# Three weight sums per Strassen step instead of four: the first made by an adding transfer in the raw slot, the last two in one operation; four raw slots and a ring of 2 KB cells

## The chip, the cores and the metric

The kernel runs on one core of a Trainium2 chip. Its time is in microseconds (us) of the device, from the first to the last instruction and what lies around them, as the median of several runs. Three runs of the kernel before gave 2356.12 to 2356.76 us, median 2356.58. One more execution was taken by the profiler, and all tables come from it. The engines have short names: PE multiplies matrices, DVE works on vectors, ACT evaluates functions and also copies, POOL and SP here mostly issue transfers (DMAs).

## What is computed

One decoder block over 256 tokens of width 4096, all in float32. Nearly all of its work is four kinds of matrix product with weights that are read once:

```python
h = rmsnorm(x, norm_w)
proj = h @ w_in                       # 4096 x 20480
u_p, z_p, u_c, b_c, c_c, z_c, g_logit = split(proj)
y_pool = causal_multiscale_pool(u_p, pool_w, pool_scale) * silu(z_p)
y_conv = causal_gated_shortconv(u_c, b_c, c_c, conv_w, conv_b) * silu(z_c)
br = [y_pool @ w_branch[0], y_conv @ w_branch[1]]      # each 2048 x 4096
gates = sigmoid(g_logit + gate_b)
x = x + (gates[0] * br[0] + gates[1] * br[1]) @ w_out  # 4096 x 4096
return rmsnorm(x, final_norm_w)
```

## The kernel before

**Numbers in two parts.** PE multiplies numbers of type fp32r, which have fewer bits than float32. Each operand is therefore split into a high part (rounded to fp32r) and a low part (what rounding took away), and each product is made of three: high by high, high by low, low by high.

**Units and steps.** The output is made in units of 256 tokens by 1024 columns: conv branch (cz, cb, cu, cc), pool branch (pz, pu), eight gate units (g), eight branch units (b), four output units (o0 to o3). A unit sums over 16 steps (a branch unit over 8). One step is one block of weights, 128 partitions by 2048 float32, 1 MB: a 2 by 2 block matrix of quarters with 512 columns each, numbered 0 to 3 along the partition's row.

A step is plain (P) or Strassen (S). P takes 8 block products of 3 matmuls, 24 in all. S takes 7, so 21, but on the weight side it needs sums of quarters, which must be formed and split into parts as well. On the side of x the sums Q3, Q5, Q6, Q7 are kept in SBUF (`sums_s`, L767). A text for each unit sets the kinds: the middle gate units follow `TEN = "PSPSSPSSPSSPSSPS"` (L42), ten S steps to six P. The whole program has 222 S steps.

**Banks.** Products with quarters 0 and 1 and the last sum go to the banks called sums, the others to four banks called shared. At a unit's end ACT copies the shared banks to the tile J (`copy_corners`, L410), DVE forms three sums there (`corner_sums`, L415: two of 128x512 and one of 128x1024), and these are added to the unit's result E or Y (`combine`, L425). For units marked late that addition is done by two DMAs of POOL, `gather` (L84): a gather reads a source and adds it to what stands at its destination.

**Preparing a step.** SP loads the block into one of `NRAW = 3` raw slots (`issue_load`, L976). `first` (L256) has ACT write the high parts into cells of the ring (`highs`, L231): four for P, quarters 0 to 2 for S. `rest` (L277) has DVE write the low parts (`lows`, L235). For S, `added` (L293) forms four sums on DVE in the tile sums, which the profile calls parts, and `split` (L301) writes their high and low parts. The ring has 15 cells; each holds a high and a low part of 512 columns, 4 KB per partition. Cells are given out in a circle and released after the last matmul that reads them.

**What sets the order.** The whole program is written out in one fixed order: every helper pins its instruction behind the one before it on its engine. `multiply` (L1021) emits a group of three matmuls; after each group `after_group` copies what is finished, lets `tick` (L1014) take a small piece of other work, and calls `pump` (L988). The pump emits the preparation of later steps, up to `AHEAD = 4` steps ahead, as long as the ring has room; it emits the load of block n as soon as block n-3 has been prepared, and on SP that load then waits until DVE is through with the slot. POOL has no computing to speak of: it issues stores, reloads and gathers, in program order.

In the profile the DVE helpers are all L61, ACT's activations L58, SP's loads L76, POOL's plain DMAs L82 and gathers L85, and the matmuls L1026.

Of the kernel before, what the change touches and what calls it, by code (L numbers as in the profile page):

```python
# [9 lines left out]
F32 = mybir.dt.float32  # L10
# [16 lines left out]
CELLS = 15  # L27
NRAW = 3
# [22 lines left out]
def hybrid_block(ctx: ExitStack, tc: tile.TileContext, x, xc, prm, rows_in, w_in, pool_w, w_branch, w_out, out):  # L51
# [49 lines left out]
    ring = blocks("ring", [P, CELLS, 2, NH], F32R)  # L101
    E = blocks("E", [P, 2, NU])
    sa = blocks("sa", [P, 8, P])
# [126 lines left out]

    def highs(cells, src):  # L231
# [7 lines left out]
    def high(cell, a=0, b=NH):  # L239
        return ring[:, cell, 0, a:b]  # L240

    def low(cell, a=0, b=NH):
        return ring[:, cell, 1, a:b]
# [4 lines left out]
    class Step:  # L248
# [7 lines left out]
        def first(self):  # L256
# [3 lines left out]
            def rounded(cells):  # L260
                self.q = self.raw.rearrange("p (i c) -> p i c", i=4)
                self.cells = cells
                if self in steps[:2]:
                    for i in range(4):
                        if self is steps[0] and i == 0:
                            copy(ring[:, cells[0], 0], self.q[:, 0])
                        else:
                            highs(cells[i:i + 1], self.q[:, i:i + 1])
                elif self.halved:
                    for i in (0, 2):  # L270
                        highs(cells[i:i + 2], self.q[:, i:i + 2])
                else:
                    highs(cells, self.q[:, 0:len(cells)])

            return [(3 if self.kind == "S" else 4, None, rounded)]

        def rest(self):  # L277
            if self.kind == "P":
                def rests(_):
                    if self in steps[:2]:  # L280
                        for i in range(4):
                            if self is steps[0] and i % 2 == 0:
                                x_low(0, 1 - i // 2)
                            lows(self.cells[i:i + 1], self.q[:, i:i + 1])
                    elif self.halved:
                        for i in (0, 2):
                            lows(self.cells[i:i + 2], self.q[:, i:i + 2])
                    else:
                        lows(self.cells, self.q)

                return [(None, None, rests)] + self.mid
            if self.kind == "S":
                def added(_):  # L293
                    q = self.q
                    add(sums[:, 0:2], q[:, 3:4].to_broadcast([P, 2, NH]), q[:, 1:3])
                    lows(self.cells[2:3], q[:, 2:3])
                    add(sums[:, 2], sums[:, 0], q[:, 2])
                    lows(self.cells[0:2], q[:, 0:2])
                    add(sums[:, 3], sums[:, 2], q[:, 0])

                def split(cells):  # L301
                    self.sum_cells = cells
                    highs(cells[0:2], sums[:, 0:2])
                    for i in (2, 3):
                        highs(cells[i:i + 1], sums[:, i:i + 1])
                    lows(cells[0:2], sums[:, 0:2])
                    lows(cells[2:4], sums[:, 2:4])

                return [(None, None, added)] + self.mid + [(4, None, split)]
            if self.kind == "B":  # L310
                def parts(cells):
                    self.cells = cells
                    highs(cells, quarters(E))
                    lows(cells, quarters(E))

                return [(4, lambda: self.unit.flags.get("base"), parts)]

            def pooled(cells):
                self.pool_cells = cells
                q = quarters(E)[:, 2 * self.g:2 * self.g + 2]  # L320
                highs(cells, q)
                lows(cells, q)

            return [(None, None, lambda _: lows(self.cells, self.q)),
                    (2, lambda: self.unit.flags.get(f"pooled{self.g}"), pooled)]

        def groups(self):
            gs = []
            if self is steps[0]:
                for k in (1, 0):  # L330
                    for n in (1, 0):
                        cell = self.cells[2 * (1 - k) + 1 - n]
                        h, l = high(cell), low(cell)
# [4 lines left out]
                        gs[-1][2] = [cell]  # L338
            elif self.kind == "P":
                for k in (1, 0):  # L340
                    for n in reversed(self.halves):
                        cell = self.cells[2 * (1 - k) + 1 - n]
                        for t in self.toks:
                            ah, al = self.op.standing(k, t)
                            gs.append([("E", t, n), [(ah, high(cell)), (ah, low(cell)), (al, high(cell))], ()])
                        if self.final:
                            gs[-1][2] = [cell]
            else:
                d, w = self.cells, self.sum_cells
                prods = {"M1": (A11, d[2], ("F", 0, 0)),  # L350
                         "N3": (Q3, d[1], ("E", 0, 0)),
                         "M2": (A12, d[0], ("E", 0, 1)),
                         "N5": (Q5, w[1], ("F", 0, 1)),
                         "N7": (Q7, w[0], ("F", 1, 0)),
                         "N6": (Q6, w[2], ("F", 1, 1)),
                         "N4": (A22, w[3], ("E", 1, 1))}
                order = ("M2", "N3", "N4", "M1", "N7", "N5", "N6") if self.closing else (
                    "M2", "N3", "M1", "N7", "N5", "N6", "N4")
                for nm in order:
                    o, cell, bank = prods[nm]  # L360
                    ah, al = self.op.entry(o)
                    mm = [(ah, high(cell)), (ah, low(cell)), (al, high(cell))]
                    gs.append([bank, mm, [cell]])
# [280 lines left out]
    def band_sums(st):  # L644
        c = st.band
        for b in range(8):
            g = b // 4
            o = shared(b // 2)[:, (b % 2) * T:(b % 2 + 1) * T]
            c0, c1 = st.cells[g], st.cells[2 + g]
            ab = (b % 4) * P, (b % 4 + 1) * P  # L650
            bands, edge = band_pool["bands"], band_pool["edge"]
            pin(nc.tensor.matmul(o, high(c0, *ab), bands[:, g], start=True, stop=False))  # L652
            pin(nc.tensor.matmul(o, low(c0, *ab), bands[:, g], start=False, stop=False))  # L653
# [593 lines left out]
```

## Time and profile before

| | busy us | share of the span | instructions |
|---|---|---|---|
| PE | 2340.7 | 99% | 10424 |
| DVE | 2217.8 | 94% | 2454 |
| ACT | 1542.9 | 66% | 1841 |
| POOL | 139.0 | 6% | 195 |
| span of the profiled execution | 2354.7 | | 28337 |
| median of three runs | 2356.58 | | |

For the profiled execution the span is what is recorded; the three timed runs lie 1.4 to 2.1 us above it, which is what surrounds the first and the last instruction. The DMA engines were busy for 71% of the span (56.7% for SP's queue, 13.7% for POOL's, the rest small).

A row for a group of instructions reads: line, engine, operation, destination <- source, shapes, count | busy us, mean ns of one | idle time of the engine just before them and what ended it. A row of a timeline begins with its start and its length in us. A row of DMA issues ends with the KB of one and the us from issue to landing. A row of a window gives the window, then for each engine its busy time and its count of instructions, then PE's granted clock, the DMA engines' share and the rate.

### The profile page before, as it was taken

How to read it: one execution, taken by the hardware profiler on the slowest of the kernel's cores; microseconds unless marked ns; L12 is line 12 of the kernel's file. 1: busy time of each engine (PE TensorE's matmuls, PEld its weight loads, DVE VectorE, ACT ScalarE, POOL GpSimd, SP SyncE). 2: the span in 40 equal slices, each digit the busy share in tenths (PEclk: the TensorE clock that was granted, in tenths of full speed). 3: DMA queues.
4: the chain of work that ended last, by engine and by line, in shares of the span. 5: the costliest groups of instructions: out<-in, count | busy, mean ns of one | idle time of the engine just before them, and what ended most of it. 6: DMA issues, size and time to landing. Idle time of an engine off the chain costs nothing.

```text
span 2354.7 us, 28337 instructions
## 1 busy us (share of the span) xinstructions
PE 2340.7 (99%) x10424; PEld 1938.7 (82%) x10424; DVE 2217.8 (94%) x2454; ACT 1542.9 (66%) x1841; POOL 139.0 (6%) x195
## 2 busy tenths in 40 slices
PE   9999999999999999999999999999999999999998
PEld 7888888888888888888888888888888888888886
DVE  8899989999979979979999999998999899999998
ACT  6666756766656666666677767677666566566664
POOL 0000000000001000100000000001101001000000
PEclk9999999999999999999999999999999999999999
DMA  9667655776656656656787787778767678767877
GB/s 351 231 234 248 217 201 215 251 232 233 222 207 216 219 196 213 220 198 222 242 258 254 256 265 246 250 267 283 258 225 247 254 247 282 250 206 263 260 255 279
DMA packets 95387, 569.44 MB, mean 242 GB/s; under 512 B 10320, under 2 KB 10576, under 8 KB 34832
## 3 DMA queue, kind: packets, MB, share of 16 engines
q1 hardware_dynamic: 69824, 485.39, 56.7%
q0 software_dynamic: 24848, 81.01, 13.7%
q8 instruction: 81, 1.33, 0.2%
q10 hardware_dynamic: 576, 1.24, 0.1%
q14 instruction: 58, 0.48, 0.1%
HBM read 521.46 MB, written 25.17 MB: 232 GB/s over the span
## 4 chain that ended last, share of the span: by engine, by line
PE 97%; DVE 1%; DMA 0%; ACT 0%; issue 0%; DVEq 0%; SPq 0%; ACTq 0%
PE sums L1026 70%; PE shared L1026 25%; PE shared L676 1%; PE shared L462 1%; DVE ring L61 1%; DMA raw<-in_w_branch_dram 0%; DVE parts L61 0%; DMA raw<-in_w_in_dram 0%; ACT ring L58 0%; DVE arena L61 0%; PE shared L652 0%; DVE J L61 0%; ACT E L58 0%; PE shared L653 0%; PE shared L655 0%
## 5 line engine op out<-in xcount | busy, mean ns | idle before, releaser
L1026 PE MATMUL sums<-ring,arena 128*128 128x512 f32 x7011 | 1640.7, 390 | 1.9 <-ACT E L58 1.1
L1026 PEld LDWEIGHTS sums<-ring,arena 128*128 128x128 f32 x7011 | 1315.3, 188 | 275.5 <-ACT E L58 1.5
L61 DVE TENSOR_TENSOR ring<-raw,ring 128x1024 fp32r<-128x1024 f32 (+2 forms) x887 | 962.2, 1104 | 70.4 <-ACT ring L58 69.5
L58 ACT ACTIVATE ring<-raw 128x1024 fp32r<-128x1024 f32 (+3 forms) x682 | 785.5, 1192 | 210.2 <-PE sums L1026 98.5
L58 ACT ACTIVATE ring<-parts 128x512 fp32r<-128x512 f32 (+1 forms) x683 | 510.4, 761 | 510.2 <-DVE parts L61 438.3
L1026 PE MATMUL shared<-ring,arena 128*128 128x512 f32 x2241 | 541.1, 389 | 0.0
L61 DVE TENSOR_TENSOR ring<-parts,ring 128x1024 fp32r<-128x1024 f32 (+1 forms) x475 | 524.5, 1146 | 8.7 <-ACT ring L58 8.7
L1026 PEld LDWEIGHTS shared<-ring,arena 128*128 128x128 f32 x2241 | 420.6, 188 | 87.3
L61 DVE TENSOR_TENSOR parts<-parts,raw 128x512 f32<-128x512 f32 x444 | 303.3, 683 | 0.0
L61 DVE TENSOR_TENSOR parts<-raw 128x1024 f32<-128x1024 f32 x222 | 270.2, 1217 | 10.9 <-DMA raw<-in_w_in_dram 6.0
L61 DVE TENSOR_TENSOR J<-J 128x512 f32<-128x512 f32 (+1 forms) x90 | 78.1, 868 | 6.0 <-ACT J L58 2.8
L1026 PE MATMUL sums<-ring,last_pair 128*128 128x512 f32 x306 | 76.2, 389 | 0.0
L58 ACT ACTIVATE J<-shared 128x512 f32<-128x512 f32 x128 | 69.5, 601 | 1.6
L1026 PEld LDWEIGHTS sums<-ring,last_pair 128*128 128x128 f32 x306 | 57.4, 188 | 11.9
L85 POOL DMA_DIRECT2D E<-J x28 | 34.2, 1463 | 479.5 <-ACT ring L58 300.1
L1026 PE MATMUL shared<-ring,last_pair 128*128 128x512 f32 x216 | 51.9, 389 | 0.0
L1026 PE MATMUL shared<-ring,side 128*128 128x512 f32 x207 | 50.7, 389 | 0.0
L1026 PEld LDWEIGHTS shared<-ring,last_pair 128*128 128x128 f32 x216 | 40.5, 188 | 8.4
L1026 PEld LDWEIGHTS shared<-ring,side 128*128 128x128 f32 x207 | 38.9, 188 | 8.1
L58 ACT ACTIVATE E<-sums 128x512 f32<-128x512 f32 x76 | 41.8, 592 | 4.5 <-PE sums L1026 2.7
L85 POOL DMA_DIRECT2D Y<-J x12 | 14.7, 1458 | 265.1 <-ACT ring L58 138.5
L58 ACT ACTIVATE E<-sums,rin 128x512 f32<-128x512 f32 x20 | 13.0, 689 | 13.9 <-PE sums L1026 13.9
(140 smaller groups left out, 645.6 us busy)
## 6 DMA issues: line engine op xcount, KB each, us to landing
raw<-in_w_in_dram SPq DMA_DIRECT2D x318, 1024.0 KB, 4.9
raw<-in_w_branch_dram SPq DMA_DIRECT2D x64, 1024.0 KB, 5.4
raw<-in_w_out_dram SPq DMA_DIRECT2D x64, 1024.0 KB, 4.8
E<-J POOLq DMA_DIRECT2D x28, 512.0 KB, 8.6
E<-in_rows_dram POOLq DMA_DIRECT2D x14, 512.0 KB, 9.8
Y<-J POOLq DMA_DIRECT2D x12, 512.0 KB, 9.3
gates_d<-E POOLq DMA_DIRECT2D x6, 1024.0 KB, 6.1
y_d<-E POOLq DMA_DIRECT2D x8, 512.0 KB, 5.2
```

Of the source, the lines that this page charges most:

```text
L58: return pin(nc.scalar.activation(dst, src, func, **kw))
L61: return pin(nc.vector.tensor_tensor(out=dst, in0=a, in1=b, op=op))
L85: return pin(nc.gpsimd.dma_start(dst, src, accum_op=ALU.add))
L462: pin(nc.tensor.transpose(shared(j)[:, i * T + t * P:i * T + (t + 1) * P], src[:, t, c:c + P], ident))
L676: pin(nc.tensor.matmul(o, a, b, start=(k, i) == (0, 0), stop=(k, i) == (3, 2)))
L1026: pin(nc.tensor.matmul(ps, lhs, rhs, start=n == 0, stop=n == u.total[b] - 1))
```

## The change

The signs of the sums change (Q5 = A21 + A22, Q7 = A21 - A11, Q3 = A12 - Q6), and with them the weight sums: three instead of four have to be formed beside the raw quarters. With the quarters w0 to w3 of a block, quarter 3 of the slot becomes w3 + w2, which is then split like a raw quarter; the tile parts holds p0 = w3 + w2 - w1, p1 = w0 - p0 and p2 = w2 - p0.

- **Loads.** Of an S block SP loads quarter 3 (256 KB) and then quarters 0 to 2 (768 KB). Then POOL adds quarter 2, read from DRAM a second time, onto quarter 3 in the slot: a gather of 256 KB. There are 222 of them.
- **High and low parts.** ACT writes the high parts of all four quarters in one activation of 128x2048 (before: three quarters, 128x1536), and those of the three sums in 128x512 and 128x1024.
- **DVE.** p0 (128x512), the low part of quarter 3 (128x512), p1 and p2 in one operation (128x1024), and later, once six cells are free, the low parts of quarters 0 to 2 (128x1536) and of the three sums (128x1536).
- **Room.** Four raw slots instead of three (for the first 16 loads the pump still counts three). The ring has 27 cells of 2 KB; high and low parts get cells of their own, 14 for an S step and 8 for a P step. parts becomes a fixed tile, sa moves, and the last unit uses raw slots where it used sums.
- **Group order.** In an S step that doesn't close a unit N5 moves ahead of N7 and N6: M2, N3, M1, N5, N6, N7, N4.

The counts of the built programs: 10424 matmuls in both; DVE tensor-tensor operations 2328 and 1908; ACT activations 1822 and 1571; DMAs on SP 484 and 706, on POOL 149 and 371.

```diff
-CELLS = 15
-NRAW = 3
+CELLS = 27
+NRAW = 4
+EARLY = 3
...
-    ring = blocks("ring", [P, CELLS, 2, NH], F32R)
+    ring = blocks("ring", [P, CELLS, NH], F32R)
...
+    parts = sb("parts", [P, 3, NH])
+    sa = sb("sa", [P, 8, P])
...
     def highs(cells, src):
         for i, c in runs(cells):
-            act(ring[:, c, 0], src[:, i])
+            act(ring[:, c], src[:, i])
-    def lows(cells, src):
-        for i, c in runs(cells):
-            sub(ring[:, c, 1], src[:, i], ring[:, c, 0].bitcast(F32))
+    def lows(to, cells, src):
+        for i, c, o in pieces(cells, to):
+            sub(ring[:, o], src[:, i], ring[:, c].bitcast(F32))
...
-            return [(3 if self.kind == "S" else 4, None, rounded)]
+            return [(4, None, rounded)]
...
-                def added(_):
-                    q = self.q
-                    add(sums[:, 0:2], q[:, 3:4].to_broadcast([P, 2, NH]), q[:, 1:3])
-                    lows(self.cells[2:3], q[:, 2:3])
-                    add(sums[:, 2], sums[:, 0], q[:, 2])
-                    lows(self.cells[0:2], q[:, 0:2])
-                    add(sums[:, 3], sums[:, 2], q[:, 0])
+                def added(to):
+                    q, d = self.q, self.cells
+                    self.lows = to
+                    sub(parts[:, 0], q[:, 3], q[:, 1])
+                    lows(to[3:4], d[3:4], q[:, 3:4])
+                    sub(parts[:, 1:3], q[:, 0:3:2], parts[:, 0:1].to_broadcast([P, 2, NH]))
                 def split(cells):
-                    self.sum_cells = cells
-                    highs(cells[0:2], sums[:, 0:2])
-                    for i in (2, 3):
-                        highs(cells[i:i + 1], sums[:, i:i + 1])
-                    lows(cells[0:2], sums[:, 0:2])
-                    lows(cells[2:4], sums[:, 2:4])
-                return [(None, None, added)] + self.mid + [(4, None, split)]
+                    self.sum_cells, self.sum_lows = cells[0:3], cells[3:6]
+                    highs(cells[0:1], parts[:, 0:1])
+                    highs(cells[1:3], parts[:, 1:3])
+                    lows(self.lows[0:3], self.cells[0:3], self.q[:, 0:3])
+                    lows(cells[3:6], cells[0:3], parts)
+                return [(4, None, added)] + self.mid + [(6, None, split)]
...
-                prods = {"M1": (A11, d[2], ("F", 0, 0)),
-                         "N3": (Q3, d[1], ("E", 0, 0)),
-                         "M2": (A12, d[0], ("E", 0, 1)),
-                         "N5": (Q5, w[1], ("F", 0, 1)),
-                         "N7": (Q7, w[0], ("F", 1, 0)),
-                         "N6": (Q6, w[2], ("F", 1, 1)),
-                         "N4": (A22, w[3], ("E", 1, 1))}
+                prods = {"M1": (A11, plain(2), ("F", 0, 0)),
+                         "N3": (Q3, plain(1), ("E", 0, 0)),
+                         "M2": (A12, plain(0), ("E", 0, 1)),
+                         "N5": (Q5, plain(3), ("F", 0, 1)),
+                         "N6": (Q6, formed(0), ("F", 1, 1)),
+                         "N4": (A22, formed(1), ("E", 1, 1)),
+                         "N7": (Q7, formed(2), ("F", 1, 0))}
                 order = ("M2", "N3", "N4", "M1", "N7", "N5", "N6") if self.closing else (
-                    "M2", "N3", "M1", "N7", "N5", "N6", "N4")
+                    "M2", "N3", "M1", "N5", "N6", "N7", "N4")
...
     def sums_s(st):
-        sub(st[:, Q5], st[:, A21], st[:, A22])
+        add(st[:, Q5], st[:, A21], st[:, A22])
         sub(st[:, Q6], st[:, Q5], st[:, A11])
-        sub(st[:, Q7], st[:, A11], st[:, A21])
-        add(st[:, Q3], st[:, A12], st[:, Q6])
+        sub(st[:, Q7], st[:, A21], st[:, A11])
+        sub(st[:, Q3], st[:, A12], st[:, Q6])
...
+        elif s.kind == "S":
+            load(r[:, 3 * NH:], s.src[:, 3 * NH:])
+            load(r[:, 0:3 * NH], s.src[:, 0:3 * NH])
+            gather(r[:, 3 * NH:], s.src[:, 2 * NH:3 * NH])
...
-            if nl < len(loaded) and (nl < NRAW or loaded[nl - NRAW].prepared):
+            ahead = EARLY if nl < 16 else NRAW
+            if nl < len(loaded) and (nl < ahead or loaded[nl - ahead].prepared):
```

The first place that the prediction speaks of is DVE at the end of an output unit whose successor begins P, S, as the gate units do too. The rows are DVE's instructions in order, with destination, sources and shape; J is the tile of the corner sums. Before, they stand like this:

```order
L61 TENSOR_TENSOR ring<-raw,ring 128x2x512 x2
L61 TENSOR_TENSOR parts<-raw 128x1024
L61 TENSOR_TENSOR ring<-raw,ring 128x512
L61 TENSOR_TENSOR parts<-parts,raw 128x512
L61 TENSOR_TENSOR ring<-raw,ring 128x2x512
L61 TENSOR_TENSOR parts<-parts,raw 128x512
L61 TENSOR_TENSOR ring<-parts,ring 128x2x512
L61 TENSOR_TENSOR ring<-parts,ring 128x512 x2
L61 TENSOR_TENSOR J<-J 128x512 x2
L61 TENSOR_TENSOR J<-J 128x1024
```

The P step is the first row, the S step the next seven, and the S step is complete before the sums in J. In the changed program DVE has at the same place:

```order
L62 TENSOR_TENSOR ring<-raw,ring 128x1024 x2
L62 TENSOR_TENSOR parts<-raw 128x512
L62 TENSOR_TENSOR ring<-raw,ring 128x512
L62 TENSOR_TENSOR parts<-raw,parts 128x1024
L62 TENSOR_TENSOR J<-J 128x512 x2
L62 TENSOR_TENSOR J<-J 128x1024
L62 TENSOR_TENSOR ring<-raw,ring 128x1536
L62 TENSOR_TENSOR ring<-parts,ring 128x1536
```

Two operations of the S step, the low parts of quarters 0 to 2 and of the sums, have moved behind the sums in J. This is so at 16 of the 30 places in the changed program where sums in J are formed.

The second place is POOL at the end of an output unit. E<-J are the two gathers that fold J into the result, E<-in_x_dram two gathers that add x to it, and the plain DMAs (L82) fetch and store other things. Before:

```order
L82 DMA sa<-m_d 128x512
L85 DMA E<-J 128x2x512 x2
L85 DMA E<-in_x_dram 128x1024 x2
L82 DMA sa<-m_d 128x512
L82 DMA Y<-in_rows_dram 128x1024
L82 DMA o_d<-E 128x2048
```

And in the changed program:

```order
L83 DMA sa<-m_d 128x512
L86 DMA raw<-in_w_out_dram 128x512 x4
L86 DMA E<-J 128x2x512 x2
L86 DMA E<-in_x_dram 128x1024 x2
L86 DMA raw<-in_w_out_dram 128x512 x2
L83 DMA sa<-m_d 128x512
L83 DMA Y<-in_rows_dram 128x1024
L86 DMA raw<-in_w_out_dram 128x512 x2
L83 DMA o_d<-E 128x2048
```

The gathers of the S blocks (raw<-in_w_out_dram) stand among the others in one line; two of them have to pass behind E<-J and E<-in_x_dram.

More of the change, by code (lines that the diff above doesn't have):

```diff
@@ L265, in rounded @@
                         if self is steps[0] and i == 0:
[L266 removed]
+                            copy(ring[:, cells[0]], self.q[:, 0])
                         else:
@@ L327, in groups, with rests, plain, formed @@
+            def rests(to):
+                self.lows = to
+                lows(to, self.cells, self.q)
+            return [(4, None, rests), (4, lambda: self.unit.flags.get(f"pooled{self.g}"), pooled)]
+        def plain(self, i):
+            return cell(self.cells[i]), cell(self.lows[i]), [self.cells[i], self.lows[i]]
+        def formed(self, i):
+            return cell(self.sum_cells[i]), cell(self.sum_lows[i]), [self.sum_cells[i], self.sum_lows[i]]
         def groups(self):
@@ L331, in groups @@
                     for n in (1, 0):
-                        cell = self.cells[2 * (1 - k) + 1 - n]
-                        h, l = high(cell), low(cell)
+                        h, l, free = self.plain(2 * (1 - k) + 1 - n)
                         for i in range(3):
@@ L672, in mix @@
                 ab = (k % 2) * T + t * P, (k % 2) * T + (t + 1) * P
-                ah, al = high(st.pool_cells[k // 2], *ab), low(st.pool_cells[k // 2], *ab)
-                h, l = high(st.cells[k]), low(st.cells[k])
+                ah, al = cell(st.pool_cells[k // 2], *ab), cell(st.pool_lows[k // 2], *ab)
+                h, l, _ = st.plain(k)
                 for i, (a, b) in enumerate(((ah, h), (ah, l), (al, h))):
                     pin(nc.tensor.matmul(o, a, b, start=(k, i) == (0, 0), stop=(k, i) == (3, 2)))
-        for q in st.cells + st.pool_cells:
+        for q in st.cells + st.lows + st.pool_cells + st.pool_lows:
             rg.release(q)
@@ L1134, in hybrid_block @@
                 opening.close()
-                sums = ctx.enter_context(tc.tile_pool(name="parts", bufs=1)).tile([P, 4, NH], F32, name="parts")
                 open_side()
@@ L1165, in hybrid_block @@
             flush()
-            rest = sums.rearrange("p (t a) n -> p t (a n)", t=2)
+            rest = slot(0)
             move(rest, xrows[:, :, 3 * NU:])
```

78 lines of the change are left out of this document (41 added, 37 removed).

## The prediction

> **What bounds the kernel now.** I read the page's first part and its chain, then PE's waits, then two windows. From the page: the span, the busy times and the shares of the chain that ended last.
>
> ```profile
> span 2354.7 us, 28337 instructions
> PE 2340.7 (99%) x10424; PEld 1938.7 (82%) x10424; DVE 2217.8 (94%) x2454; ACT 1542.9 (66%) x1841; POOL 139.0 (6%) x195
> PE 97%; DVE 1%; DMA 0%; ACT 0%; issue 0%; DVEq 0%; SPq 0%; ACTq 0%
> ```
>
> PE is idle for 2354.7 - 2340.7 = 14.0 us in all, and the chain is 97% PE. What it waits for (engine, tile, line, releaser: us, times, longest):
>
> ```profile
> PE shared L873 <- DVE warm L869: 1.1, 1, 1.1
> PE sums L1026 <- ACT E L58: 1.1, 1, 1.1
> PE sums L1026 <- DVE ring L774: 0.8, 1, 0.8
> ```
>
> Three waits, 3.0 us. Two stand in the head; the third is for ACT's copy of a result. PE never waits for prepared weights, though DVE is busy for 94%. The windows show how close that is: a gate unit with ten S steps, and the last 55 us.
>
> ```profile
> 1260.95:1341.19 80.24, 80.24 (x355) 66.44 (x355) 80.17 (x89) 56.03 (x66) 5.28 (x6) 1.00 0.78 256
> 2300.00:2355.00 55.00, 43.72 (x193) 35.85 (x192) 44.96 (x58) 25.31 (x35) 1.80 (x3) 0.94 0.72 274
> ```
>
> The gate unit has 10 x 21 + 6 x 24 = 354 matmuls in 80.24 us: 0.2267 us each without a gap, 5.02 us a step on average. DVE is busy for 80.17 of it, so here it just keeps up. Of the 14.0 idle us of PE, 11.3 lie in the last window (55 - 43.72).
>
> **The change: PE.** The list stays at 10424 matmuls of the same shapes; only groups swap places. Nothing goes from the path there.
>
> **DVE.** Groups by shape:
>
> ```profile
> L61 DVE TENSOR_TENSOR parts<-raw 128x1024 f32<-128x1024 f32 x222 | 270.2, 1217 | 10.9 <-DMA raw<-in_w_in_dram 6.0 <-DMA raw<-in_w_out_dram 4.8
> L61 DVE TENSOR_TENSOR parts<-parts,raw 128x512 f32<-128x512 f32 x444 | 303.3, 683 | 0.0
> L61 DVE TENSOR_TENSOR ring<-parts,ring 128x1024 fp32r<-128x1024 f32 x413 | 487.2, 1216 | 8.7 <-ACT ring L58 8.7
> L61 DVE TENSOR_TENSOR ring<-raw,ring 128x512 fp32r<-128x512 f32 x298 | 201.2, 684 | 22.3 <-ACT ring L58 21.9
> L61 DVE TENSOR_TENSOR ring<-raw,ring 128x1536 fp32r<-128x1536 f32 x8 | 14.0, 1750 | 0.7 <-ACT ring L58 0.7
> L61 DVE TENSOR_TENSOR ring<-raw,ring 128x1024 fp32r<-128x1024 f32 x530 | 632.9, 1217 | 14.4 <-ACT ring L58 14.1
> ```
>
> An S step before: 1217 + 684 + 683 + 1217 + 683 + 2 x 1216 = 6916 ns. After: p0 683, low of quarter 3 684, p1 and p2 1217, two lows of 1536 columns 2 x 1750: 6084 ns. That is 832 ns less, x 222 = 185 us: DVE goes from 2217.8 to about 2033 us, 86%, and in the gate unit from 80.2 to about 72. PE waited for none of it, so on the path it is worth nothing; at most it could touch the three waits, and none of them is for an S step.
>
> **ACT.** Here too the work gets a little lighter.
>
> ```profile
> L58 ACT ACTIVATE ring<-raw 128x1536 fp32r<-128x1536 f32 x198 | 293.9, 1485 | 138.1 <-PE sums L1026 57.8 <-issue 27.3 <-DMA raw<-in_w_in_dram 25.1
> L58 ACT ACTIVATE ring<-raw 128x2048 fp32r<-128x2048 f32 x51 | 97.7, 1920 | 50.2 <-PE sums L1026 29.6 <-PE shared L676 12.8 <-DMA raw<-in_w_in_dram 4.8
> L58 ACT ACTIVATE ring<-parts 128x1024 fp32r<-128x1024 f32 x205 | 217.5, 1061 | 256.2 <-DVE parts L61 226.7 <-PE sums L1026 16.2 <-PE shared L1026 12.4
> L58 ACT ACTIVATE ring<-parts 128x512 fp32r<-128x512 f32 x478 | 298.4, 632 | 254.0 <-DVE parts L61 211.6 <-PE sums L1026 13.0 <-PE shared L1026 12.5
> ```
>
> Plus 1920 - 1485 = 435, minus one 632 ns activation: about 0.2 us less per S step, 44 us in all, beside other work. Idle time that ends with PE is ACT waiting for room in the ring: preparation runs ahead of PE. The new ring holds 27 x 2 = 54 KB, 13.5 pairs for 15; an S step takes 7 pairs as before.
>
> **The gather: latency.** The trace of before doesn't show this. Issues with KB and median us to landing, and POOL's durations of an adding DMA that reads DRAM (min/median/max ns):
>
> ```profile
> raw<-in_w_in_dram SPq DMA_DIRECT2D x318, 1024.0 KB, 4.9
> raw<-in_w_in_dram SPq DMA_DIRECT2D x8, 256.0 KB, 5.4
> sa<-m_d POOLq DMA_DIRECT2D x8, 256.0 KB, 5.2
> E<-in_rows_dram POOLq DMA_DIRECT2D x14, 512.0 KB, 9.8
> L85 POOL DMA_DIRECT2D E<-in_rows_dram x14: 860/876/913, 1222.9 to 1685.6; - x14
> ```
>
> Before, an S slot is held 4.9 + 6.9 = 11.8 us of a round of 3 x 5.02 = 15.1: 3.3 us spare. After: the load of quarter 3 lands (5.4), the gather lands, DVE works 6.1. For the gather the ends are 5.2 (256 KB, plain) and 9.8 (adding from DRAM, twice the size); I take 5.2, the same size. Sum 16.7 of a round of 4 x 5.02 = 20.1: 3.4 spare, about what there was; with 9.8 it is 21.3, 1.2 too long. But P steps share the round with 4.9 + 2.4 = 7.3, so a unit's mean is (10 x 16.7 + 6 x 7.3) / 16 = 13.2, with 6.9 spare, and with 9.8 it is 16.1, with 4.0 spare. So the fourth slot covers the gather; with three slots, 16.7 would stand against 15.1. The wait for it is ACT's, whose activation of the four quarters comes first. Behind that on ACT stand the copies out of the banks, E<-sums and J<-shared, and PE waited once, 1.1 us, for one of those; a gather later than the cover would thus reach PE by two ways.
>
> [...]
>
> **The gather: POOL and the DMA engines.** POOL issues 222 x 0.88 = 195 us more, 139 to 334, 14%. For the engines' time two windows bound it: one inside a pair of gathers E<-J, one with loads alone.
>
> ```profile
> 1201.00:1203.00 2.00, 2.00 (x11) 1.65 (x10) 2.00 (x4) 1.26 (x2) 0.70 (x2) 1.00 1.15 177
> 1242.50:1244.50 2.00, 2.00 (x11) 1.65 (x10) 2.00 (x3) 2.00 (x4) 0.00 (x0) 1.00 0.90 352
> q1 hardware_dynamic: 69824, 485.39, 56.7%
> q0 software_dynamic: 24848, 81.01, 13.7%
> ```
>
> 256 KB at 177 GB/s is 1.48 us, or 1.70 with the share of 1.15; at 352 GB/s and 0.90 it is 0.67. I take 1.48, since it adds. A gate unit goes from 0.78 to 0.78 + 10 x 1.48 / 80.24 = 0.96 (0.86 to 0.99), the program from 0.71 to 0.85.
>
> **The sum.** 2354.7 us of the profiled span, minus nothing, plus about 1 us for single steps that come late (below), and the 1.9 us that the median of the runs, 2356.58, lies above the span: 2357.5. A measurement can tell about 0.2%, 4.7 us, from no change.
>
> **Rival 1, slower: POOL's queue.** The gathers of the S blocks are issued in program order with the others. At the end of an output unit POOL's timeline reads:
>
> ```profile
> 2105.13 2.48 POOL L85 DMA_DIRECT2D E<-J  x2 [34.68 <-ACT ring L58]
> 2111.18 0.89 POOL L85 DMA_DIRECT2D E<-in_x_dram  x1 [3.57 <-DMA E<-J]
> 2120.73 0.85 POOL L85 DMA_DIRECT2D E<-in_x_dram  x1 [8.67 <-DMA E<-J]
> ```
>
> And over all gathers of L85, their landing:
>
> ```profile
> DMA to landing us min/median/max: 4.9/9.9/15.2
> ```
>
> POOL is held for 16.5 us (2105.13 to 2121.6), and the order puts two S gathers behind that. At the 20 pairs E<-J or Y<-J a gather behind lands up to 15.2 - 5.2 = 10 us late. The other direction counts as well: a gather waits on POOL until SP's load has a slot and has landed, and stores, reloads and E<-J stand behind it. What covers a late gather is the spare time of the round (6.9 on the mean, 3.4 for a single S) and DVE's lead over PE, 3.7 us (next rival's rows: the sums are ready at 1275.4, PE takes them from 1279.15). With 10.6 us of cover the pairs cost nothing, and of the holds of 16.5, if they fall evenly, 36% reach 2.9 us beyond on average: 3 x 1.0 = 3 us. With 7.1, the pairs give 20 x 0.29 x 1.45 = 8 us and the holds 3 x 0.57 x 4.7 = 8, together 16. Between them 9: 2366 us. It decides from a lateness of 7 to 11 us. For it speaks that PE has no idle time to absorb a wait; against it, the lighter DVE, which catches up 0.8 us per S step.
>
> **Rival 2, slower: J ahead of the S step's low parts.** In the gate unit's start, by engine:
>
> ```profile
> 1269.63 2.20 PE L1026 MATMUL shared<-ring,side 128*128 128x512 f32 x9
> 1271.67 6.28 PE L1026 MATMUL sums<-ring,arena 128*128 128x512 f32 x27
> 1279.15 2.20 PE L1026 MATMUL shared<-ring,side 128*128 128x512 f32 x9
> ...
> 1273.70 1.55 ACT L58 ACTIVATE J<-shared 128x512 f32<-128x512 f32 x3
> ...
> 1272.99 2.42 DVE L61 TENSOR_TENSOR ring<-parts,ring 128x1024 fp32r<-128x1024 f32 x3
> 1275.33 2.67 DVE L61 TENSOR_TENSOR J<-J 128x512 f32<-128x512 f32 x3
> ```
>
> The shared banks close at 1271.67; the first P step takes PE 24 x 0.2267 = 5.44 us, to 1277.11, and the second matmul of the S step needs a low part at 1277.34. Before, these were written ahead of J. Now ACT's copies (at best until 1272.4), J (2.6) and the low parts (1.75) come first: 1276.75, 0.6 us in time. If ACT's copies stand behind an activation of 1.92 us, it is 1.3 late; at 16 such places 21 us at most, at half of it 10: 2367. It decides once ACT or DVE is 0.6 us late there. Against it: without ACT's wait for parts, which held the copies until 1273.70 before, they come earlier.
>
> **Rival 3, slower: the DMA engines are full in the gate units.** It decides from (1 - 0.78) x 80.24 / 10 = 1.77 us a gather. At 2.0 the unit takes 1.03 x 80.24 = 82.6; six such units are 14 us longer: 2371. For it speaks 1.70, not far below; against it, that 1.70 is my highest price. [...]
>
> **Rival 4: the change doesn't do what it says.** If long operations are cut where the ring wraps, DVE gains less. The counts, 2328 to 1908 tensor-tensor operations, are 420 of the 2 x 222 = 444 that uncut steps would save, so little of that. PE wouldn't feel it: 2357.
>
> **Rival 5, faster.** All three waits gone: 2353.5. More than 0.2% would need a third of PE's 14.0 idle us, most of it the closing norm, which stays.
>
> **Chances.** Forecast 0.54, rival 4 0.03: within 0.2% 0.57. POOL 0.19, J 0.11, DMA engines 0.10: slower 0.40. Faster 0.03. The range goes from 2353.5 to 2377, which holds the high end of rival 1 (2373), rival 3 and most of rival 2's (2378).
>
> **What would show it.** Right: PE's matmuls without waits in the gate units (80.24 us each), DVE near 2033 us, POOL near 334, the gate units' DMA share near 0.96. Rival 1: PE waiting for DVE's ring just behind an E<-J, with DVE waiting for the DMA raw<-in_w_out_dram or raw<-in_w_in_dram. Rival 2: PE waits of under 1.5 us some 5 us into a unit, and DVE's J rows ahead. Rival 3: gate units longer than 80.24 with the share at 1.0 throughout. Wrong altogether: landing times of the gather above 10 us outside the pairs.

## The result, and the profile after

The changed kernel takes 2398.81 us (median of four runs, 2391.04 to 2401.42) beside 2356.35 for the kernel before: 1.0174 times, 95% interval 1.0158 to 1.0190. It is 42 us slower; the forecast was no measurable change, 2357.5, and the range ended at 2377. The profiled execution spans 2398.0 us, 43.3 more than the one before. First the page's first part, the chain that ended last and the two large DMA queues:

```profile
span 2398.0 us, 28884 instructions
PE 2355.6 (98%) x10424; PEld 1940.0 (81%) x10424; DVE 2085.4 (87%) x2034; ACT 1496.9 (62%) x1590; POOL 328.0 (14%) x417
PE 78%; DMA 8%; DVE 7%; issue 4%; ACT 2%; POOL 1%; SPq 0%; DVEq 0%; ACTq 0%; POOLq 0%
q1 hardware_dynamic: 101792, 485.40, 56.0%
q0 software_dynamic: 56816, 139.22, 28.4%
```

The chain now runs through DMAs and DVE as well. DVE is 132 us lighter and POOL 189 heavier. PE's waits, which were 3.0 us in three places:

```profile
PE sums L1045 <- DVE ring L62: 26.4, 22, 3.9
PE sums L1045 <- ACT ring L59: 1.7, 2, 1.3
PE shared L887 <- DVE warm L883: 1.1, 1, 1.1
PE sums L1045 <- DVE ring L788: 1.1, 1, 1.1
PE sums L1045 <- ACT E L59: 0.9, 1, 0.9
```

They add up to 31.2 us, 28.2 more, nearly all for parts that DVE hadn't written yet. The other 14.9 us are in PE's busy time, with the same 10424 matmuls. Four windows at or right behind the longest stops (the last three numbers: granted clock, DMA share, GB/s) show a part of the reason:

```profile
1430.90:1434.30 3.40, 3.40 (x10) 2.63 (x9) 3.37 (x5) 1.19 (x3) 0.00 (x0) 0.51 1.00 393
2161.30:2168.10 6.80, 4.57 (x11) 3.62 (x12) 6.76 (x10) 6.18 (x9) 0.00 (x0) 0.50 0.69 214
2250.10:2256.90 6.80, 5.50 (x13) 4.34 (x14) 6.77 (x6) 6.57 (x9) 0.00 (x0) 0.50 0.68 216
2338.80:2342.20 3.40, 3.01 (x7) 2.44 (x8) 3.40 (x4) 3.37 (x5) 0.85 (x1) 0.50 0.58 207
```

Behind these stops PE gets half its clock (0.50 or 0.51 of it in the windows), for 3.4 or 6.8 us. It is busy for 16.5 us in the four windows; at half speed that costs some 8 of the 14.9 us. The rest is not traced here. The waits before the four are 2.5, 1.3 and 3.0, 0.4 and 3.0, and 3.9 us.

Where the stops come from, seen in the chain (start, us, what), in a gate unit and at the end of output unit o0:

```profile
1235.46 2.43 DVE ring L62 x3
...
1237.91 8.36 DMA raw<-in_w_in_dram
...
1246.89 9.10 DMA raw<-in_w_in_dram
...
2140.37 4.78 issue
...
2145.86 12.02 DMA raw<-in_w_out_dram
```

The first row is DVE's work that frees a slot, the second a load that starts right behind it and took 8.4 us, the third the gather behind that, 9.1. At 2145 POOL has just issued the second gather of x, after waiting 4.8 us for a gather E<-J to land, and the S block's gather behind it takes 12.0 us. That issue on POOL, DVE's low parts of quarters 0 to 2 for the gate unit's block, and in PE's timeline the stops that follow, two in the gate unit and two at the output unit:

```profile
2145.16 0.86 POOL L86 DMA_DIRECT2D E<-in_x_dram  x1 [4.79 <-DMA E<-J]
1259.84 1.75 DVE L62 TENSOR_TENSOR ring<-raw,ring 128x1536 fp32r<-128x1536 f32 x1
1261.65 1.43 PE L1045 MATMUL sums<-ring,arena 128*128 128x512 f32 x5 [0.93 <-DVE ring L62]
1267.39 1.45 PE L1045 MATMUL sums<-ring,last_pair 128*128 128x512 f32 x5 [0.67 <-DVE ring L62]
2160.00 0.50 PE L1045 MATMUL sums<-ring,arena 128*128 128x512 f32 x1 [1.31 <-ACT ring L59]
2163.53 2.50 PE L1045 MATMUL sums<-ring,arena 128*128 128x512 f32 x5 [3.03 <-DVE ring L62]
```

The landing times over the whole program (KB, median us); in the kernel before it was 4.9 for a load of 1024 KB:

```profile
raw<-in_w_in_dram SPq DMA_DIRECT2D x150, 1024.0 KB, 7.0
raw<-in_w_in_dram SPq DMA_DIRECT2D x168, 768.0 KB, 6.8
raw<-in_w_in_dram SPq DMA_DIRECT2D x176, 256.0 KB, 5.9
raw<-in_w_in_dram POOLq DMA_DIRECT2D x168, 256.0 KB, 6.0
```

### The profile page after: what moved, and what is told of

It reads as the page before. It is cut to its first block, busy times and chain, and to the rows that moved or that the text cites. A ratio compares the mean times of both kernels' runs of the same rounds, so it can differ in the third digit from the quotient of the medians.

```text
span 2398.0 us, 28884 instructions
## 1 busy us (share of the span) xinstructions
PE 2355.6 (98%) x10424; PEld 1940.0 (81%) x10424; DVE 2085.4 (87%) x2034; ACT 1496.9 (62%) x1590; POOL 328.0 (14%) x417
## 3 DMA queue, kind: packets, MB, share of 16 engines
q0 software_dynamic: 56816, 139.22, 28.4%
## 4 chain that ended last, share of the span: by engine, by line
PE 78%; DMA 8%; DVE 7%; issue 4%; ACT 2%; POOL 1%; SPq 0%; DVEq 0%; ACTq 0%; POOLq 0%
PE sums L1045 57%; PE shared L1045 19%; DMA raw<-in_w_in_dram 6%; DVE ring L62 4%; DMA raw<-in_w_out_dram 2%; DVE parts L62 2%; ACT ring L59 2%; PE shared L690 1%; PE shared L476 1%; POOL E L86 1%; ACT J L59 0%; ACT E L59 0%; DVE J L62 0%; PE shared L666 0%; PE shared L667 0%
## 5 line engine op out<-in xcount | busy, mean ns | idle before, releaser
L62 DVE TENSOR_TENSOR ring<-raw,ring 128x512 fp32r<-128x512 f32 (+3 forms) x904 | 1086.2, 1220 | 133.3 <-ACT ring L59 57.0
L59 ACT ACTIVATE ring<-raw 128x1024 fp32r<-128x1024 f32 (+3 forms) x661 | 882.3, 1370 | 321.8 <-DMA raw<-in_w_in_dram 98.4
L59 ACT ACTIVATE ring<-parts 128x1024 fp32r<-128x1024 f32 (+1 forms) x451 | 372.5, 840 | 415.5 <-DVE parts L62 307.4
L62 DVE TENSOR_TENSOR ring<-parts,ring 128x1536 fp32r<-128x1536 f32 (+2 forms) x258 | 391.8, 1530 | 14.6 <-ACT ring L59 14.6
L86 POOL DMA_DIRECT2D raw<-in_w_in_dram x168 | 145.3, 865 | 1332.3 <-DMA raw<-in_w_in_dram 597.4
L62 DVE TENSOR_TENSOR parts<-raw,parts 128x1024 f32<-128x1024 f32 x222 | 270.5, 1219 | 0.0
L62 DVE TENSOR_TENSOR parts<-raw 128x512 f32<-128x512 f32 x222 | 152.4, 687 | 61.6 <-DMA raw<-in_w_out_dram 28.3
L86 POOL DMA_DIRECT2D raw<-in_w_out_dram x31 | 27.7, 893 | 219.1 <-DVE ring L62 97.4
L86 POOL DMA_DIRECT2D raw<-in_w_branch_dram x23 | 20.2, 877 | 245.7 <-DMA raw<-in_w_branch_dram 86.5
```

The costliest lines, as they stand in the source:

```text
L59: return pin(nc.scalar.activation(dst, src, func, **kw))
L62: return pin(nc.vector.tensor_tensor(out=dst, in0=a, in1=b, op=op))
L86: return pin(nc.gpsimd.dma_start(dst, src, accum_op=ALU.add))
```

## The experiments

Each was made from the changed kernel unless another is named.

**Bytes or order.** e4 cuts the bytes and keeps every issue and wait; e2 and e3 take other gathers out of the way; e7 takes all of them apart.

```diff
 e4:
-            gather(r[:, 3 * NH:], s.src[:, 2 * NH:3 * NH])
+            gather(r[:, 3 * NH:3 * NH + 64], s.src[:, 2 * NH:2 * NH + 64])
 e2, output units:
-            return gap(2) + [lambda: row(0), lambda: row(1)] + gap(12) + [start] + gap(8) + [
+            return gap(14) + [lambda: row(0), lambda: row(1)] + [start] + gap(8) + [
 e3, gate units:
-            items = (rescale(d) if u.late else gap(1)) + [lambda: bias(0), lambda: bias(1)] + gap(12) + [
+            items = (rescale(d) if u.late else gap(1)) + (gap(2) if u.late else [lambda: bias(0), lambda: bias(1)]) + gap(12) + [
 e7, combine, the end of a unit, gate units, output units:
+            if u.late and not u.urgent:
+                gather(d4[:, 0], q[:, 0])
+                u.second = lambda: gather(d4[:, 1], q[:, 1])
...
+            items[5] = u.second
...
+            items = (rescale(d) if u.late else gap(1)) + [lambda: bias(0)] + gap(6) + [lambda: bias(1)] + gap(10) + [
...
+            return gap(14) + [lambda: row(0)] + gap(6) + [lambda: row(1), start] + gap(10) + [
```

> The changed kernel, but each gather of an S block adds 64 of the 512 columns (32 KB in place of 256 KB); the other columns of the sum are not formed. The order on POOL and all waits stay. Theory A2 (bytes on the DMA engines): loads land within 5 to 6 us again and nearly all stalls go, 2357 to 2365 us. Theory A1 (order on POOL): the gathers still stand behind the others, the stalls at the output units stay: 2372 to 2385 us.

> The changed kernel, but in the output units the two gathers that add x are issued 12 small pieces of work later (some 16 us), when the gathers E<-J have landed, so that POOL doesn't stand still with the gathers of S blocks behind it. Theory A1 (order on POOL): the three stalls at the ends of output units, 4.3 to 4.8 us each with 2 to 3 us of a lower clock behind them, go: about 2376 us. Theory A2 (the DMA engines are full for a while after each burst of adding DMAs, wherever it stands): the stalls only move, 2392 to 2400 us.

> The changed kernel without the two gathers that add the bias rows in the seven late gate units; their gates lack the bias. Theory A2 (a burst of 1 MB of adding DMA makes the loads and gathers behind it land late): the stalls near the ends of the gate units go, about 10 us of waits and 2 us of lower clock: 2384 to 2388 us. Theory A1 (order on POOL): these two hold POOL for some 2 us only, so little changes: 2395 to 2400 us.

> The changed kernel with the other gathers taken apart: the second E<-J or Y<-J five pieces of work behind the first (some 7 us), the two of the bias six pieces apart, those of x in the output units 14 pieces later and seven apart. Same bytes, same S gathers. If bursts of adding DMA are what makes the chain of load and gather late: PE waits under 12 us, 2358 to 2372 us. If the mean load of the DMA engines is too high anyway: 2385 us or more.

Measured: e4 2360.97 us, 1.0015 times the kernel before (1.0005 to 1.0025); PE's waits for the ring fall from 26.4 to 3.1. So the order on POOL, unchanged in e4, costs little by itself, and so does DVE's order at J, which e4 keeps as well. e2 2387.49 (1.0111 to 1.0143), e3 2386.62 (1.0099 to 1.0145), e7 2385.82 (1.0111 to 1.0146): each gains 11 to 13 us. For e3 that is what its first theory said; e2 lies between its two ranges, and e7 at the lower edge of its second.

**Occupancy or the gather's own landing; adding or bytes.** e9 puts a quarter of each gather into the slot and the rest into a tile that nobody reads; e13 makes that rest a plain transfer.

```diff
 e9:
-            gather(r[:, 3 * NH:], s.src[:, 2 * NH:3 * NH])
+            gather(r[:, 3 * NH:3 * NH + 128], s.src[:, 2 * NH:2 * NH + 128])
+            gather(idle, s.src[:, 2 * NH + 128:3 * NH])
 e13:
+            move(idle, s.src[:, 2 * NH + 128:3 * NH])
```

> The changed kernel with the gather of each S block cut in two: 128 of the 512 columns go into the slot as before (64 KB; the other columns of the sum are not formed), 384 columns (192 KB) go into a tile that nobody reads (26 cells in the ring to make room). Bytes on the DMA engines as in the changed kernel, one more issue on POOL per S step. If the gather's own landing of some 6 us is what is too long: 2358 to 2370 us. If the engines' occupancy does it, by late loads: 2388 us or more, with loads landing in 7 us and more.

> e9 with the second part (192 KB per S step into a tile that nobody reads) as a plain transfer of POOL, not an adding one. Bytes, issues and order are e9's. If it is the adding that fills the DMA engines (in the changed kernel an added MB costs 6.2 us of all 16 engines, a loaded one 2.8): 2362 to 2385 us. If it is the bytes: 2405 us or more.

e9: 2414.55 us (1.0222 to 1.0256). e13: 2386.42 (1.0093 to 1.0127), 28 us less for the same bytes, and just above its first range. Landing times of POOL's gathers into raw slots, in the changed kernel, e9, e13 and e4:

```profile
DMA to landing us min/median/max: 3.9/6.0/12.1
DMA to landing us min/median/max: 2.6/5.5/12.2
DMA to landing us min/median/max: 2.6/4.8/10.9
DMA to landing us min/median/max: 2.3/3.8/9.7
```

And of SP's loads into them, in the same order:

```profile
DMA to landing us min/median/max: 2.6/6.6/14.1
DMA to landing us min/median/max: 2.7/6.6/12.6
DMA to landing us min/median/max: 2.6/6.0/12.8
DMA to landing us min/median/max: 2.6/5.2/13.1
```

In e9 a gather of 64 KB still takes 5.5 us beside the rest of the bytes, and the time is worse, with one more issue per step and a cell less. So e9 didn't make the gather's landing short, and it can't tell that landing from the engines' occupancy. What the rows show is that gathers and loads land sooner together as the adding (e13) and then the bytes (e4) go. One difference beside the adding remains between e9 and e13: the transfers into the one tile wait on POOL for the one before, 251 us in e9 and 151 in e13. POOL's queue in e9 and then e13:

```profile
q0 software_dynamic: 88784, 139.24, 29.3%
```

```profile
q0 software_dynamic: 71024, 139.24, 24.7%
```

By the shares of POOL's queue after and before, the added 58.2 MB (139.22 - 81.01) of the changed kernel took 0.284 x 2398.0 - 0.137 x 2354.7 = 358 us of all 16 engines, 6.2 us per MB or 1.61 us per gather; SP's loads took 0.560 x 2398.0 / 485.4 = 2.8 us per MB. An added MB cost 2.2 times a loaded one here.

**DVE's order at J.** e15 moves one operation, e14 does it in e7.

```diff
 split:
-                    lows(self.lows[0:3], self.cells[0:3], self.q[:, 0:3])
 added, at its end:
+                    lows(to[0:3], d[0:3], q[:, 0:3])
```

> The changed kernel with nothing but the one operation of DVE moved: the low parts of quarters 0 to 2 right behind p1 and p2, so that they no longer wait until the ring has six free cells, and the raw slot is given back earlier. If the slot held for the ring is a large part of the lateness: 2376 to 2384 us, as e14 gained 18 us over e7. If the move helps only where the other gathers are apart: 2392 us or more.

> e7 (four slots, the other gathers apart) with the same operation moved as in e12. e7's stops are mostly of late loads and gathers, few of them behind J: 2375 to 2386 us. If the order behind J were what costs the time in the changed kernel, it would come to 2365 us or less.

e15: 2381.44 us (1.0091 to 1.0122), 17 less by this alone. e14: 2367.40 (1.0026 to 1.0052), 18 less than e7, between its two ranges. The expectation of e15 blamed room in the ring; by the order in the two traces 27 of the 222 operations moved, and 19 of them pass the sums in J. DVE around such a place, changed kernel, and then e15:

```profile
1198.45 1.22 DVE L62 TENSOR_TENSOR parts<-raw,parts 128x1024 f32<-128x1024 f32 x1
1200.90 2.68 DVE L62 TENSOR_TENSOR J<-J 128x512 f32<-128x512 f32 x3 [1.23 <-ACT J L59]
1203.50 1.75 DVE L62 TENSOR_TENSOR ring<-raw,ring 128x1536 fp32r<-128x1536 f32 x1
```

```profile
1193.52 1.22 DVE L62 TENSOR_TENSOR parts<-raw,parts 128x1024 f32<-128x1024 f32 x1
1194.65 1.75 DVE L62 TENSOR_TENSOR ring<-raw,ring 128x1536 fp32r<-128x1536 f32 x1
1196.32 2.67 DVE L62 TENSOR_TENSOR J<-J 128x512 f32<-128x512 f32 x3
```

In the changed kernel DVE stands still 1.23 us for ACT's copies into J, with the low parts behind it, and it is through with the raw slot 5.6 us after p1 and p2 (1199.67 to 1205.25); in e15 1.7 us after (1194.74 to 1196.40). DVE's waits for J over the program, again the changed kernel and e15 (us, times, longest):

```profile
DVE J L62 <- ACT J L59: 36.7, 27, 2.6
```

```profile
DVE J L62 <- ACT J L59: 13.9, 9, 2.6
```

PE hardly stops at that place itself; its stops in this unit come later, at 1261 and 1267, so the account is that the lead lost there is missing when a burst of DMA comes. Whether it is lost by the slot held longer or by DVE's own standing still, no run separates. And in e14 the gate unit runs without a gap at a DMA share of 0.96:

```profile
1181.00:1261.24 80.24, 80.24 (x356) 66.46 (x355) 74.15 (x69) 54.84 (x56) 13.98 (x16) 1.00 0.96 290
```

The landing times of e14, gathers and then loads, are those of the changed kernel:

```profile
DMA to landing us min/median/max: 3.9/6.2/12.5
DMA to landing us min/median/max: 2.6/6.5/12.4
```

**Slots.** e8 has three slots (its last unit then parks results in slots that overlap, so the end of its output is not computed), e10 five with a ring of 23 cells and `TAIL = 2`, e11 adds e7's edits, e12 also e15's.

> The changed kernel with three raw slots. The round is then 15.05 us in a gate unit, and an S slot is held for 5.9 + 6.0 + 6.1 = 18.0 us by the landing times measured after the change, a P slot for 7.0 + 2.4 = 9.4: a mean of 14.8. If the slots cover the gather, as the prediction has it, nothing is left for a burst and the time is 2420 to 2500 us. If the fourth slot does little, it stays at 2395 to 2405 us.

> The changed kernel with a fifth raw slot, paid for with four cells of the ring (23) and a last stage of two plain steps in place of three. All transfers and their order stay. If the chain load, gather, DVE is too long for four slots only at bursts, a round of 25.1 us covers it: PE waits under 8 us, 2357 to 2368 us. If the ring or the order on POOL is what is short: 2385 us or more.

> e10 with the other gathers taken apart as in e7. If bursts on top of the chain are the whole cause: 2356 to 2362 us, no better than the kernel before, since PE then has its 10424 matmuls and nothing to wait for.

> e11 (five slots, the other gathers apart) with one operation of DVE moved: the low parts of quarters 0 to 2 are written right behind p1 and p2, ahead of the sums in J, and no longer behind them. Rival 2 of the prediction (J ahead of the low parts) explains the 1.07 us that e11 shows once in nearly every unit: 13 of them go, 14 us, to 2380 to 2385 us. If the stop comes from the ring of 23 cells, it stays: 2395 to 2399 us.

e8: 2615.05 us (1.1079 to 1.1112), worse than the theory's 2500: the fourth slot is worth over 200 us here. e10: 2405.23 (1.0190 to 1.0220), in its second range; e11: 2397.56 (1.0157 to 1.0187), against expectation. The stops for DMA in the gate units are gone, but one of 1.07 us, by the starts of neighbouring matmuls, stands at the start of nearly every unit. e11, PE and DVE:

```profile
1216.76 0.73 PE L1048 MATMUL sums<-ring,arena 128*128 128x512 f32 x2 [0.91 <-DVE ring L62]
...
1212.37 2.67 DVE L62 TENSOR_TENSOR J<-J 128x512 f32<-128x512 f32 x3
1214.96 1.75 DVE L62 TENSOR_TENSOR ring<-raw,ring 128x1536 fp32r<-128x1536 f32 x1
```

That is rival 2 as the prediction drew it, low parts behind J, PE waiting for them. e12 takes it away: 2380.35 (1.0077 to 1.0107), 17 less, as expected. What e12 still lacks to 2357 was not taken further; the smaller ring is the likely cause, not shown.

**DVE in place of the gather.** e1 lets DVE add quarter 2 to quarter 3 before ACT's high parts; e5 orders that so that DVE needn't wait for ACT (it also puts p1 and p2 ahead of the low part of quarter 3); e6 adds to e5 a gather per S step into a tile that nobody reads.

```diff
 e1:
+                if self.kind == "S":
+                    add(self.q[:, 3], self.q[:, 3], self.q[:, 2])
 e5:
+                    add(self.q[:, 3], self.q[:, 3], self.q[:, 2])
+                    highs(cells[0:3], self.q)
+                    highs(cells[3:4], self.q[:, 3:4])
 e6:
+                gather(idle, s.src[:, 2 * NH:3 * NH])
```

> The changed kernel, but the first weight sum is an addition of DVE in the raw slot (128x512) in place of the adding DMA, and the block is one load of 1 MB. Signs, three sums, four slots, the ring of 2 KB cells and the order of the J sums stay. Theory A (the 222 gathers cost the time: they come late, because POOL or the DMA engines are occupied): back to 2355 to 2359 us, PE waits near 3 us, DVE about 2085 + 222 x 0.68 = 2237 us. Theory C (the rest of the change costs it: J ahead of the low parts, the ring, the slots): 2385 us or more.

> As e1 (DVE adds quarter 2 to quarter 3, no gather of S blocks), but ordered so that DVE needn't wait for ACT: ACT writes the high parts of quarters 0 to 2 first and that of quarter 3 after it; DVE does the addition, p0, p1 and p2, and then the low part of quarter 3. If e1's 2641 us came from DVE and ACT waiting for one another at each S step and not from the three sums, the slots or the ring: 2355 to 2360 us, DVE waiting for ACT's ring for less than 100 us in all. If the rest of the change costs time (theory C): 2380 us or more.

> As e5, with a gather of 256 KB per S block as in the changed kernel, at the same place on POOL, but into a tile of its own that nobody reads (the ring has 26 cells to make room). It occupies POOL and the DMA engines and delays nothing by dependency. If occupancy alone costs the time (loads come too late because the engines are full): 2375 us or more. If it takes the chain of load and gather in one slot round: 2355 to 2363 us, with loads that land in 6 to 7 us as in the changed kernel.

e1 and e5 missed their first ranges by far and lie in the open ranges of theory C, and e6 in that of occupancy, but not for the reasons given there. e1: 2641.63 us (1.1185 to 1.1218). DVE's first wait there:

```profile
DVE ring L62 <- ACT ring L59: 279.6, 211, 4.4
```

Addition, high part and low part of quarter 3 go back and forth between the two at each S step. e5: 2409.16 (1.0203 to 1.0237). A gate unit of e5:

```profile
1223.04:1306.34 83.30, 81.81 (x355) 65.98 (x354) 81.02 (x79) 55.84 (x66) 5.30 (x6) 1.00 0.73 246
```

It takes 83.3 us, with DVE busy for 81.0: with the addition an S step needs nearly as much DVE as before the change (6084 + 683 = 6767 ns by the prediction's durations, against 6916), so DVE is the bound again. Three sums without the gather are no gain in this form. e6: 2429.55 (1.0296 to 1.0327); since DVE bounds its base, it doesn't tell the two theories apart. Its added gathers are also not free of waits, as was meant: all go into one tile, and POOL stood still for the one before 178 times, 1246 us in all.

**What is left.** e16 moves the load of the norm's weights in e14's output units ahead of x; e17 is e16 with ten S steps in four units that have nine.

```diff
 e16:
-            return gap(14) + [lambda: row(0)] + gap(6) + [lambda: row(1), start] + gap(10) + [
+            return gap(7) + [start] + gap(6) + [lambda: row(0)] + gap(6) + [lambda: row(1)] + gap(11) + [
 e17:
-        u = in_unit(f"cu{c}", base, lambda u: rescale(Y), NINE, dst=Y)
+        u = in_unit(f"cu{c}", base, lambda u: rescale(Y), TEN, dst=Y)
...
-        in_unit(f"cc{c}", base + 2 * HALF, c_epi, NINE_A).urgent = lambda: mul(E, E, Y)
+        in_unit(f"cc{c}", base + 2 * HALF, c_epi, TEN).urgent = lambda: mul(E, E, Y)
```

> e14 with the load of the last norm's weights (Y<-in_rows_dram, plain, on POOL) in the output units issued ahead of the gathers that add x. In e14 it stood behind a gather of an S block that waited for its load, DVE waited 9.8 us for it and PE 7.0: the one long stop that is left. Without it, and the 3 us of lower clock behind it: 2355 to 2360 us, the time of the kernel before.

> e16 with ten S steps in place of nine in four units (cu0, cc0, cu1, cc1), which DVE's 12% of idle time may now carry: 12 matmuls fewer, 2.7 us of PE, at four more gathers and four more loads of 512 KB. If nothing new is late: 2 to 3 us under e16, at or just below the kernel before. If the DMA engines are too full: not faster than e16.

e16: 2367.70 us (1.0030 to 1.0055), e17: 2366.71 (1.0023 to 1.0049). Neither beats the kernel before, nor e14 by more than the noise. e14's stop of 7 us is gone in e16, but PE's waits still have

```profile
PE sums L1048 <- DVE ring L62: 6.5, 3, 2.5
```

three stops: one of 1.8 us in the head, and 2.2 and 2.5 us in the output units (at 2139 and 2313), where gathers of E, of x and of S blocks meet. The mean granted clock of e16's profiled execution is 0.997; it is 0.994 in the changed kernel and 0.999 in the kernel before. No version tried beats the kernel before, in which PE is busy for 99% of the span.

## Why the prediction was wrong

- **PE bounds, its list is unchanged: right.** No run came under the time of the kernel before.
- **DVE: right in sign, somewhat large.** 185 us forecast, 132 measured. I added the durations of single instructions; neighbours overlap by some 0.08 us (in e15's rows 1194.65 + 1.75 is 1196.40, and the next starts at 1196.32), so fewer and longer ones save less. In the two traces the durations of all DVE instructions add up to 175 us less, and the overlap of neighbours to 43 us less.
- **The gather's price on engines and POOL: right.** 1.48 us forecast, 1.61 measured; POOL 334 and 328 us; share of the program 0.85 and 0.85 (56.0 + 28.4 and small ones), of a gate unit 0.96 and 0.93 (1181 to 1263, stretched by stops).
- **The sum for the raw slot: this step failed.** "I take 5.2, the same size. Sum 16.7 of a round of 4 x 5.02 = 20.1: 3.4 spare", with 6.9 on the unit's mean, and from there "So the fourth slot covers the gather". It used landing times of the kernel before, at a share of 0.71 to 0.78, beside a share of 0.96 that the next paragraph worked out. Measured medians make 5.9 + 6.0 + 6.1 = 18.0, still within the round; in the burst of the gate unit, from the load's start at 1237.91 to the end of the slot's last reader at 1261.59, it is 8.4 + 0.6 + 9.1 + 5.6 = 23.7, over three us more than the round. A mean hides that. The sum also let DVE's 6.1 us run without a gap, where the slot's last reader stands behind J: 5.5 us from p1 and p2 to its end at those 19 steps, 1.7 elsewhere. Longer landings alone don't cost the time: e14 has them too. Nor does J's order alone: e4 has it. What costs, by these runs, is late landings in bursts together with a chain that has no slack there. e15, which moves the low parts ahead of J, takes 17 of the 42 us away, e7, which takes the other gathers apart, 13, both together (e14) 31, though every byte and the share of 0.96 stay. The last 11 of e14 stand at one output unit, a stop of 7.0 us and the halved clock towards its end and behind it (0.50 from 2311.4 to 2321.6, with PE busy for 5.9 us of that).
- **The cost of a stop was undersized.** I priced stops at their own length. Of the 43.3 us, 28.2 are waits and some 8 the halved clock behind them (0.50 or 0.51 in the four windows, with PE busy for 16.5 us).
- **Rival 1 (POOL's queue)** had the place right: the three longest groups of stops are at the ends of the output units, with a gather that takes 12 us to land in the slot. But e4 shows that order alone, without the bytes, costs under 5 us, and in the changed kernel's trace a gather of an S block is issued 0.7 us (median) and at most 3.5 us after the load of its quarter 3 has landed: POOL is hardly ever what it waits for.
- **Rival 2 (J ahead of the low parts)** was real, and its price right where DVE's lead is short (1.07 us a unit in e11, forecast "1.3 late"). In the changed kernel the low parts came just in time for PE, as worked out; the harm came later, by the slots or by DVE's lead, which I had not followed.
- **Rival 3 (DMA engines full)**: the mean share of a gate unit never reached 1 (0.93). What bound was the landing time in stretches where it is near 1 (0.96 to 1.05 between 1210 and 1246), against a chain without slack there.

## What to carry to other kernels

When a change raises the load of a shared resource, work out the waits with the latencies of the new load, not with those of the old profile: here the mean share rose from 0.71 to 0.85 and the landing of a load from 4.9 to 7.0 us. Follow a buffer from its load to its *last* reader and ask what stands ahead of that reader in its engine's order; one operation moved ahead of a wait gave back 17 us. And where PE has no slack, count the lowered clock behind a stop too: the four longest groups of stops here cost more than their length, with 3.4 or 6.8 us behind each at 0.50 or 0.51 of the clock.

## What the hardware showed

Adding DMAs from DRAM into SBUF took 6.2 us of all engines per MB (POOL's queue, the changed kernel less the one before), plain loads of SP 2.8. e9 and e13 differ in 43.6 MB (192 KB in each of 222 steps) that are added or only moved: 0.293 x 2415.9 - 0.247 x 2386.8 = 118 us of all engines, 2.7 us per MB for the adding alone. In the changed kernel, with stops by the starts of neighbouring matmuls, PE's clock fell to a half for 3.4 us after a stop of 2.7 us (at 1427; 0.51) and for 6.8 us around the end of two close together, 4.8 in all (at 2158; 0.50), and not after one of 2.0 (at 1177; 1.00 from 1176 to 1186). After one of 4.0 us (at 2335; 0.50) it was 3.4 us again: the longer stop brought no longer stretch there.
